# A two-level Winograd matmul with GELU: late groups taken two at a time on one block of A

## The chip, the cores and the metric

The kernel runs on one core of a Trainium2 chip. The metric is the device time of the kernel in microseconds (us), the median of several runs. A core has TensorE (PE: matmuls; PEld: loads of their stationary operand), VectorE (DVE), ScalarE (ACT), GpSimd (POOL) and SyncE (SP). GpSimd and SyncE issue the transfers here. Matmuls add up into PSUM, which has 8 banks of 128 x 512 float32; all other tiles lie in SBUF.

## The reference

```python
a: 4096 x 4096 float32, b: 4096 x 4096 float32
x = np.matmul(a, b)
return 0.5 * x * (1 + np.tanh(np.sqrt(2 / np.pi) * (x + 0.044715 * x**3)))
```

A full product of two square matrices, and GELU (tanh form) of each element. The kernel rounds A and B to fp16 and checks their sizes on the way; a slower general path stands behind that check and is not taken with these inputs.

## The kernel before

**Two levels of Winograd's scheme.** A is cut into four quadrants A11 to A22, and so is B. Seven products P1 to P7 of quadrants or of sums of quadrants give the four quadrants of the output:

```
S1 = A21+A22   S2 = S1-A11   S3 = A11-A21   S4 = A12-S2
T1 = B12-B11   T2 = B22-T1   T3 = B22-B12   T4 = B21-T2
P1 = A11*B11   P2 = A12*B21  P3 = S4*B22    P4 = A22*T4   P5 = S1*T1   P6 = S2*T2   P7 = S3*T3
C11 = P1+P2    U = P1+P6     V = U+P5       C12 = V+P3    C21 = U+P7+P4   C22 = V+P7
```

Each quadrant of C is worked in tiles of 512 rows by 512 columns. A *group* is one tile position (mb, nb) in all four quadrants at once: 4 x 4 = 16 groups, 0 to 15, each with the seven products. A product of a group is (512 x 2048) times (2048 x 512). `products` (L558, matmul on L563) does an *uncut* one: 4 quarters of the inner dimension x 4 row tiles x 4 matmuls of 512 columns. A *cut* one is done by Winograd's scheme once more (`split`, `stage`, `part_pe`, matmul on L955): 7 parts x 2 row tiles x 8 matmuls of 256 columns. It needs sums of its A operand (`inner_sum`, L883: sums "5", "7", "6", "3"; with a *base* that an earlier group of the block has left in place only "5", "7", "3"), sums of its B operand (`made_here`, `made_stored`: four each; none for `fetched` pieces), and copies and adds of half banks between its four stages (L968, L972). The stages are: part 1; parts 2, 5; parts 6, 7; parts 3, 4. Part p writes the quadrant of the product's four banks that `WHERE` (L55) names: part 3 the right half of banks 0 and 1, part 4 the left half of banks 2 and 3, part 1 also banks 2 and 3. Where `bits` is set, the first matmul of each row tile of part 1 is widened to 512 columns.

**What is cut.** `RAW_CUT` names the cut products of the raw groups 1 to 6 (B comes from the input and its sums are made and stored, `raw_group` L1344). `GROUPS` (L117) does it for groups 7 to 15: per product f (pieces of B fetched), m (B sums made in place), ms (made and stored for later), um (uncut, pieces made), and uncut if it isn't named. `late_group` (L1530) runs them one after another. A group has eight banks as two sets X and Y; two different products, such as P1 on X and P2 on Y, run interleaved stage by stage (`both`, L1627). Results leave the banks by ScalarE copies (L1166), VectorE adds (`add_bank`, L1172) and GELU (L1150). A cut P4 at the end of some groups is held back (`pending`) and run beside the next group's P1 or P4.

**Memory.** SBUF is managed by hand as 28 *cells* of 128 x 2048 fp16 (512 KB): 0 to 15 are B's four slots, 16 to 19 are called SB, 20 to 23 SA, 24 to 27 ST (the staging tiles), beside four slots of four cells for A's raw quadrants, and 15 *smalls* of 128 x 512 float32. In the late groups SA holds S1, ST holds S3, and S2 and S4 lie in SB and in A21's slot; the 16 cells of B serve fetches, B sums and inner A sums. When a row block changes (groups 7 and 11), `turn_quad` (L1185) loads the next block of A, transposes it on VectorE and sums squares on ScalarE (L1206).

**The order of the work.** Every operation is first put on record with its engine, an assumed cost (`COST`, `MOVE`), what it reads and what it writes. `Plan.schedule` (L206) then plays the program through with these costs: TensorE takes its operations in the order of the program, and each other engine takes the ready operation that is due first, waiting for a nearly ready one that is due sooner. `LAG` (0.2 us) is added between engines, and `MARGIN` (0.6 us) behind a transfer that VectorE or ScalarE waits for. `emit` writes the instructions in that order, and on the chip each engine keeps to it.

Of the kernel before, what the change touches and what calls it, by code (L numbers as in the profile page):

```python
# [16 lines left out]
P = 128  # L17
# [50 lines left out]
MARGIN = 0.6  # L68
# [21 lines left out]
def modes_of(tail=None, early=None, first4=None, **kw):  # L90
    got = {name: mode for mode, names in kw.items() for name in names.split()}
    return {**got, **{k: v for k, v in (("tail", tail), ("early", early), ("first4", first4)) if v}}


def bases_of(all_modes):
    got = {}
    for gs in (tuple(range(N_RAW, 8)), (8, 9, 10, 11), (12, 13, 14, 15)):
        early = [g for g in gs if all_modes[g].get("early") == "start"]
        turn = gs[-1] in TURNS
        for name in NAMES:  # L100
            if turn and (name in ("P2", "P6") or early and name in ("P1", "P5")):
                continue
            own = [g for g in gs if not (name == "P3" and (g in TURNS or g in early))]
            found = []
            while own and all_modes[own[-1]].get(name, "u") in ("f", "m", "ms"):
                found.append(own.pop())
            if len(found) > 1:
                for g in found:
                    got[g, name] = "made"
                got[found[-1], name] = "make"  # L110
    return got
# [16 lines left out]
TURNS = {7: 2, 11: 3}  # L128
# [191 lines left out]
def half_path(  # L320
# [105 lines left out]
    def turn_a(quad, c, h=None):  # L426

        x = slice(0, NX) if h is None else slice(h * NX // 2, (h + 1) * NX // 2)
        if (quad, c) == THIRD:
            n = NX // RT  # L430
            parts = [(slice(i * n, (i + 1) * n), staged[quad, c][i]) for i in range(x.start // n, x.stop // n)]
        else:
            parts = [(x, staged[quad, c][:, x, :])]
        for x, src in parts:
            transpose(a_slot[quad], c, x, src)

    def transpose(slot, c, x, src):
        dst = a_phys[slot, c].bitcast(U32).rearrange("p jj (mb q) -> p jj mb q", q=Q)
# [368 lines left out]

    def new_small():
        return free_small.pop(0)
# [21 lines left out]
    def fetch_unit(nb, name, q):  # L831
        x = new_cell()
        dma("POOL", cell(x), unit(nb, name)[:, q, :], [("u", nb, name, q)], [c(x)], "unit")
# [16 lines left out]


# [31 lines left out]
    def inner_sum(op, x, y, t=None):  # L883
        t = new_cell() if t is None else t
# [55 lines left out]
    def part_pe(z, p):  # L940
# [22 lines left out]
        if p in z.sum and p != "6" and z.last:  # L963
            free_cells.append(z.sum.pop(p))
# [9 lines left out]
    def stage(z, k):  # L974
# [22 lines left out]
        elif k == 2:  # L997
            part_pe(z, "2")
            x5 = z.sum["5"]
            part_pe(z, "5")  # L1000
            if z.last:
                free_cells.remove(x5)
# [182 lines left out]
    def turn_quad(mb, quad, slot, pairs):  # L1185
# [3 lines left out]
        for h in range(2):  # L1189
# [9 lines left out]
            for cc in range(CH):  # L1199
                src = s.rearrange("p x (c r) -> p c x r", c=CH)[:, cc]  # L1200
                x = slice(h * n, (h + 1) * n)
                dve("turn", lambda cc=cc, x=x, src=src: transpose(slot, cc, x, src), toks, [("a", slot, cc, h)])
            f = new_small()
            for x in range(n):
                r = h * n + x
                act("weigh", lambda x=x, r=r, s=s, f=f: nc.scalar.activation(  # L1206
                    small[f].bitcast(F16)[:, : 2 * RUN], s[:, x, :], ACT.Square, accum_out=t[:, kh, r : r + 1]),
                    toks, [("rows", ih), ("f", f)], batch=("w", mb, quad, h), slack=60.0)
            free_small.append(f)
# [134 lines left out]
    def raw_group(gi, keep_units, makes, fetch=(), next_nb=None, turn=None, pending=None):  # L1344
# [47 lines left out]
        if turn:  # L1392
# [4 lines left out]
            turn_quad(turn, "11", slots["a"]["21"], (24, 26))  # L1397
# [23 lines left out]
        if turn:  # L1421
            turn_quad(turn, "12", slots["a"]["11"], (24, 26))
# [16 lines left out]
        if turn:  # L1439
            turn_quad(turn, "21", slots["a"]["12"], (24, 26))  # L1440
# [37 lines left out]
        def p4_ends():  # L1478
            if turn:
                turn_quad(turn, "22", slots["a"]["22"], (24, 26))  # L1480
# [46 lines left out]
    sets, held_sums = {"X": 0}, []  # L1527
    BASE = bases_of(GROUPS)

    def late_group(gi, modes, turn=None, pending=None):  # L1530

        mb, nb = groups[gi]
        new_mb = gi == N_RAW or groups[gi - 1][0] != mb
        last = gi == LAST
        X, Y = sets["X"], 1 - sets["X"]
        cut = {name for name in NAMES if modes.get(name, "u") in ("f", "m", "ms")}
        p4_first = bool(turn) or "first4" in modes
        if p4_first:
            cut.discard("P4")
        tail_v = "P7" in cut or "P3" in cut and modes.get("tail") == "v" or "P4" in cut  # L1540
        tail_v = tail_v or pending is not None and not p4_first
        if gi == N_RAW:
            for q in range(QPH):
                copy_quarter(ST[q], raw("21"), q)
        elif new_mb:
            block(SA, 1, raw("21"), raw("22"))
        if new_mb or not held_sums:
            block(SB, -1, blk(SA), raw("11"))
        s3 = ST
        if new_mb and gi != N_RAW:  # L1550
            block(ST, -1, raw("11"), raw("21"))
        def early():
            k = new_unit()
            turn_quad(groups[gi][0] + 1, "11", slots["a"]["21"], (k[0], k[2]))
            free_cells.extend(k)

        held_sums.clear()
        s4_in_slot = not turn and modes.get("early") != "start"
        if modes.get("early") == "start":
            early()  # L1560
        if s4_in_slot:
            if new_mb:
                s4 = raw("21")
                for q in range(QPH):
                    dst, toks = a_quarter(s4, q)
                    combine2(dst, toks, a_quarter(raw("12"), q), a_quarter(blk(SB), q), -1)
            held_sums.append(gi)
        if turn:
            k = new_unit()
            pairs = (k[0], k[2])  # L1570

        def fourth():
            if not s4_in_slot:
                block(SB, -1, raw("12"), blk(SB))
        source = {
            "P1": raw("11"), "P2": raw("12"), "P5": blk(SA), "P6": blk(SB), "P7": blk(s3), "P3": raw("21") if s4_in_slot else blk(SB), "P4": raw("22")
        }

        def work(name, s, fresh, done=None, bits=False, lead=None, seen=None):
# [5 lines left out]
            z = split(s, source[name], b, bits, BASE.get((gi, name)), lead)  # L1585
            if seen is not None:
                seen.append(z)
            return stages_of(z, done)

        p1, u, v, y = {}, {}, {}, {}  # L1590
        alone = not {"P1", "P2"} & cut
        keep_p1 = not alone or "P6" in cut

# [24 lines left out]
        def p5_done(i):  # L1618
            if tail_v and p4_first:
# [3 lines left out]
            elif tail_v:  # L1623
                v[i] = new_small()
                add_bank(u[i], Y, i, v[i])

        def both(xs, ys):  # L1627
# [264 lines left out]
```

## Time and profile before

| | |
|---|---|
| median of 3 runs | 1497.44 us (1496.33 to 1498.01) |
| profiled execution | 1500.4 us, of which span 1498.5 us |
| mean granted clock of TensorE | 0.998 |
| moved by DMA | 388.76 MB, mean 259 GB/s |
| full-length sums of L871 on VectorE (128 x 2048 fp16) | 600 |

The span runs from the first to the last instruction of one profiled execution. "Busy" is the union of an engine's instructions; a matmul's row has its whole passage through the array as its length (379 ns for 512 columns, 273 ns for 256), while the next one starts much earlier, so that prices of matmuls are taken from start to start. A row of a group reads: line, engine, operation, output <- inputs, shape, count | busy us, mean ns of one | idle time of the engine just before, and what ended it. A row of a waiting list: engine, tile and line that waited <- what it waited for: us in all, times, longest. A row of the chain or of the timeline begins with its start and its length in us.

### The profile page before, as it was taken

To read this page: it belongs to the slowest core of one execution; us is meant where nothing else is said; L and a number is where in the kernel's file an instruction comes from. 1 tells how busy PE (TensorE), PEld (TensorE's weight loads), DVE (VectorE), ACT (ScalarE), POOL (GpSimd) and SP (SyncE) were. 2 spreads that over 40 slices of the span, in tenths; PEclk is the share of its full clock that TensorE was granted. 3 is DMA by queue.
4 is the path that set the end of the run, shared out by engine and by line. 5 is a ranking of instruction groups with operands and counts; after the bars stand their busy time and mean duration, and the time that the engine had idled before them with its cause. 6 is when DMAs were issued, how large, how long until landed. Compare 5 with 4: busy or idle time off the path is not lost.

```text
span 1498.5 us, 26219 instructions
## 1 busy us (share of the span) xinstructions
PE 1483.8 (99%) x9886; PEld 967.4 (65%) x9886; DVE 1207.5 (81%) x1476; ACT 708.8 (47%) x1606; POOL 452.6 (30%) x822
## 2 busy tenths in 40 slices
PE   9999999999999999999999999999999999999997
PEld 4444554444445446555665888887765778888886
DVE  2598778246499889686799999998699889998887
ACT  5445246363954645546663242436654234242433
POOL 7766342451204415212330212122331112112220
PEclk9999999999999999999999999999999999999999
DMA  9999799999979999997997777889997747698974
GB/s 177 193 204 224 135 247 314 292 279 268 249 269 250 284 356 254 309 264 239 252 330 297 269 265 241 299 272 215 305 283 288 259 141 264 209 336 279 327 257 182
DMA packets 200918, 388.76 MB, mean 259 GB/s; under 512 B 20304, under 2 KB 110416, under 8 KB 200784
## 3 DMA queue, kind: packets, MB, share of 16 engines
q0 software_dynamic: 139296, 231.79, 65.3%
q1 hardware_dynamic: 61488, 155.22, 27.5%
q8 instruction: 79, 1.29, 0.3%
q14 instruction: 55, 0.45, 0.1%
HBM read 315.62 MB, written 155.19 MB: 314 GB/s over the span
## 4 chain that ended last, share of the span: by engine, by line
PE 90%; DMA 5%; POOL 2%; DVE 1%; ACT 1%; issue 1%; DVEq 0%; ACTq 0%; POOLq 0%
PE acc L563 47%; PE acc L955 43%; DMA stage<-in_a_dram 2%; DMA bR<-k_unit 2%; POOL bR L465 1%; POOL stage L465 1%; DVE bR L871 0%; POOL aD L465 0%; DVE y L1172 0%; DMA out_dram<-y 0%; ACT stage L474 0%; DMA aD<-in_a_dram 0%; DMA bR<-in_b_dram 0%; ACT y L1150 0%; ACT y L1206 0%
## 5 line engine op out<-in xcount | busy, mean ns | idle before, releaser
L563 PE MATMUL acc<-bR,aT 128*128 128x512 f16 x1792 | 393.6, 379 | 1.0 <-DVE y L1172 0.6
L871 DVE TENSOR_TENSOR bR<-bR 128x2048 f16<-128x2048 f16 (+1 forms) x292 | 344.7, 1203 | 47.1 <-PE acc L955 23.6
L789 POOL DMA_DIRECT2D bR<-k_unit x258 | 143.7, 559 | 629.7 <-PE acc L955 359.3
L563 PE MATMUL acc<-bR,aD 128*128 128x512 f16 x1472 | 322.4, 379 | 0.0
L563 PEld LDWEIGHTS <-aT 128*128 128x128 f16 x1856 | 181.6, 98 | 215.0 <-issue 1.6
L955 PE MATMUL acc<-bR 128*128 128x256 f16 x2640 | 307.3, 273 | 1.5 <-ACT y L968 1.5
L955 PEld LDWEIGHTS <-bR 128*128 128x128 f16 x2640 | 258.3, 98 | 33.6 <-issue 1.6
L563 PEld LDWEIGHTS <-aD 128*128 128x128 f16 x1568 | 153.3, 98 | 182.5 <-DVE aD L548 1.2
L1172 DVE TENSOR_TENSOR y<-acc,y 128x512 f32<-128x512 f32 x324 | 209.0, 684 | 36.0 <-ACT y L1166 14.7
L789 POOL DMA_DIRECT2D bR<-in_b_dram x288 | 155.5, 545 | 252.5 <-DMA bR<-in_b_dram 102.2
L955 PE MATMUL acc<-bR,aT 128*128 128x256 f16 (+1 forms) x1696 | 201.0, 274 | 0.0
L968 ACT COPY y<-acc 128x256 f32<-128x256 f32 x220 | 81.6, 372 | 238.2 <-PE acc L955 235.4
L955 PEld LDWEIGHTS <-aT 128*128 128x128 f16 x1696 | 166.0, 98 | 24.4
L1150 ACT ACTIVATE y<-y 128x512 f32<-128x512 f32 x200 | 119.9, 626 | 109.0 <-DVE y L1172 108.7
L1240 ACT ACTIVATE y<-bR 128x1024 bf16<-128x1024 f16 x128 | 129.8, 1052 | 66.0 <-DVE y L1245 51.9
L1245 DVE TENSOR_TENSOR y<-y 128x1024 bf16<-128x1024 bf16 x120 | 82.1, 686 | 41.6 <-ACT y L1240 40.1
L955 PE MATMUL acc<-bR,aD 128*128 128x256 f16 (+1 forms) x944 | 110.9, 273 | 0.0
L955 PE MATMUL acc<-bR,stage 128*128 128x256 f16 (+1 forms) x880 | 105.7, 274 | 0.0
L955 PEld LDWEIGHTS <-aD 128*128 128x128 f16 x944 | 92.4, 98 | 12.1
L955 PEld LDWEIGHTS <-stage 128*128 128x128 f16 x880 | 86.1, 98 | 15.1
L871 DVE TENSOR_TENSOR bR<-aT 128x2048 f16<-128x2048 f16 x66 | 80.3, 1217 | 18.2 <-PE acc L563 18.2
L1166 ACT COPY y<-acc 128x512 f32<-128x512 f32 x80 | 45.9, 586 | 103.2 <-PE acc L563 65.4
(89 smaller groups left out, 1223.4 us busy)
## 6 DMA issues: line engine op xcount, KB each, us to landing
bR<-k_unit POOLq DMA_DIRECT2D x258, 512.0 KB, 7.0
out_dram<-y SPq DMA_DIRECT2D x252, 256.0 KB, 7.0
k_unit<-bR SPq DMA_DIRECT2D x112, 512.0 KB, 8.8
bR<-in_b_dram POOLq DMA_DIRECT2D x384, 128.0 KB, 6.9
k_piece<-bR SPq DMA_DIRECT2D x40, 512.0 KB, 4.7
bR<-in_a_dram POOLq DMA_DIRECT2D x64, 256.0 KB, 8.9
stage<-in_a_dram POOLq DMA_DIRECT2D x48, 256.0 KB, 7.7
bR<-k_piece POOLq DMA_DIRECT2D x24, 512.0 KB, 7.7
```

The source lines that it names most:

```text
L465: nc.gpsimd.dma_start(out=dst, in_=src)
L563: nc.tensor.matmul(acc, sa[:, j // 2, i * P : (i + 1) * P, j % 2], sb[:, j, :], start=start and j == 0, stop=stop and j == 3, skip_group_c ...
L789: return plan.add(queue, COST[queue], lambda: eng.dma_start(out=dst, in_=src), r=r, w=w, size=MOVE[what] * SPREAD, weight=weight, **kw)
L871: nc.vector.tensor_tensor(out=dst, in0=xa, in1=ya, op=ALU.add if op > 0 else ALU.subtract)
L955: nc.tensor.matmul(PS[s][i][:, :] if wide else PS[s][i][:, w * HC : (w + 1) * HC], sa[:, j // 2, r * P : (r + 1) * P, j % 2], rhs(j, wide) ...
L968: act(cost, lambda: nc.scalar.copy(out=d, in_=x), [xt] if xt else [], [dt])
L1150: act("gelu", lambda: nc.scalar.activation(t, t, ACT.Gelu_apprx_tanh), [("f", f)], [("f", f)])
L1166: act("copy", lambda: nc.scalar.copy(out=sm(f), in_=bank(s, i)), [], [("f", f), ("p", s, i)])
L1172: dve("add", lambda: nc.vector.tensor_tensor(out=sm(g), in0=bank(s, i), in1=sm(f), op=ALU.add), [("f", f)], [("f", g), ("p", s, i)])
L1240: act("square", lambda t=t, src=src: nc.scalar.activation(t, src, ACT.Square), [c(cx)], [("f", f)], slack=60.0)
L1245: dve("add16", lambda t=t, u=u: nc.vector.tensor_tensor(out=u, in0=u, in1=t, op=ALU.add), [("f", f)], [("f", e)], slack=60.0)
```

## The change

Groups 8 to 15 are taken as four pairs, (8,9), (10,11), (12,13), (14,15), by a new function `late_pair`; `late_group` becomes `lone_group` and is left for group 7 alone. Both groups of a pair have the same rows of A. The pair goes through P1, P2, P6, P5, P3, P7, P4, and at each step runs that product of both groups interleaved, the first group on bank set 0 and the second on bank set 1. Where both are cut, they share the A sums: the first makes "5" and "7", the second makes "6" over the cell of "5", and "3" over "6"; the second group runs part 5 before part 2. Bases are kept for P4 and P7 alone. S2 is made at the start of each pair in one place and overwritten by S4 ahead of P5. S3 takes A21's slot, so the four staging cells and the rest, 20 cells, are free for B; three of them (`EXTRA`) become six more smalls, which leaves 17. In three pairs (`PARK`) U is stored to DRAM ahead of P3 and fetched back ahead of P7. The next block of A is turned in groups 7 and (10,11), into whichever block is done with. The tables of what is cut are new, and `MARGIN` is 0.2 instead of 0.6. Group 7 no longer copies S3 into the staging cells (L877).

```diff
-MARGIN = 0.6
+MARGIN = 0.2
...
 def bases_of(all_modes):
     got = {}
...
+    for a, b in ((8, 10), (12, 14)):
+        for name in ("P4", "P7"):
+            if all(all_modes[g].get(name, "u") in ("f", "m", "ms") for g in (a, a + 1, b, b + 1)):
+                got[a, name], got[b, name] = "make", "made"
     return got
...
-RAW_MAKES = {4: ("P1", "P4", "P3"), 5: ("P2",)}
-RAW_CUT = {4: "P7", 5: "P7 P3", 6: "P7", 2: "", 1: "P7"}
+RAW_MAKES = {4: ("P1", "P4"), 5: ("P4",), 6: ("P3",)}
+RAW_CUT = {4: "P3", 5: "P3", 6: "P7", 2: "", 1: "P3"}
 GROUPS = {
-    7: modes_of(m="P1 P6", ms="P7", tail="v"),
-    8: modes_of(f="P7", m="P3 P4 P6", ms="P5", um="P2"),
-    9: modes_of(f="P3", m="P1 P4 P5 P6 P7", ms="P2"),
-    10: modes_of(m="P1 P2 P3 P5 P7", ms="P6", early="end"),
-    11: modes_of(m="P1 P2 P6 P7", tail="v"),
-    12: modes_of(m="P4 P6 P7", ms="P5", tail="v"),
-    13: modes_of(f="P7", m="P1 P2 P3 P4 P5 P6"),
-    14: modes_of(f="P3", m="P2 P6 P7", ms="P1 P4 P5"),
-    15: modes_of(f="P2 P6", m="P1 P4 P5 P7", ms="P3", tail="v", first4=True),
+    7: modes_of(m="P1 P5 P6", um="P2 P4", tail="v"),
+    8: modes_of(m="P1 P2 P3 P4 P6 P7", ms="P5"),
+    9: modes_of(m="P4 P5 P7", ms="P2 P6", um="P3"),
+    10: modes_of(f="P4", m="P1 P2 P3 P6", ms="P5"),
+    11: modes_of(m="P1 P2 P3 P4 P5"),
+    12: modes_of(f="P3", m="P1 P4 P5 P6 P7", ms="P2"),
+    13: modes_of(f="P4", m="P1 P2 P5 P7", ms="P3 P6"),
+    14: modes_of(f="P3", m="P4 P7", ms="P1 P2 P5 P6"),
+    15: modes_of(f="P4", m="P1 P2 P5 P6 P7", ms="P3"),
 }
+EXTRA = (13, 14, 15)
+OWN = True
+TWO = True
+TEMPS = ()
+SLACK = 60.0
+PARK = (8, 12, 14)
-TURNS = {7: 2, 11: 3}
+TURNS = {7: 2, 10: 3}
...
         elif k == 2:
-            part_pe(z, "2")
             x5 = z.sum["5"]
-            part_pe(z, "5")
+            for p in "25" if z.first else "52":
+                part_pe(z, p)
...
+    def late_pair(ga, turn):
+
+        gs = (ga, ga + 1)
...
+        if groups[ga - 1][0] != mb:
+            fill("S1", 1, "21", "22")
+            fill("S2", -1, "S1", "11")
+            at["S3"] = at["21"]
+            fill("S3", -1, "11", "21")
+        else:
+            fill("S2", -1, "S1", "11")
...
+        def both(name, fresh, dones, bits):
+            lists, cuts, lead = [], [], None
+            for s in range(2):
+                gi, mode = gs[s], GROUPS[gs[s]].get(name, "u")
...
+                b = {"f": fetched, "m": made_split, "ms": made_stored}[mode](nb, name)
+                shared = is_cut(0, name) and is_cut(1, name)
+                z = split(s, source[name], b, bits(s), BASE.get((ga, name)) if shared else None, lead)
+                lead = z if shared else None
+                lists.append(stages_of(z, lambda i, s=s: dones(s, i)))
+                cuts.append(s)
...
+        def p7_done(s, i):
+            add_bank(v[s][i], s, i)
+            if is_cut(s, "P4"):
+                add_bank(u[s][i], s, i)
+            out_of(gs[s], i, 1, 1, v[s][i])
...
+        both("P1", lambda s: True, p1_done, uncut("P2"))
+        new_a("11", "11")
...
+        both("P2", cut("P2"), p2_done, uncut("P6"))
+        both("P6", cut("P6"), p6_done, uncut("P5"))
...
+        fill("S2", -1, "12", "S2")
+        new_a("21", "12")
+        both("P5", cut("P5"), p5_done, uncut("P3"))
+        if ga in PARK:
+            park()
+        new_a("22", "S1")
+        both("P3", cut("P3"), p3_done, lambda s: False)
+        new_a("12", "S2")
+        if ga in PARK:
+            unpark()
+        both("P7", lambda s: True, p7_done, uncut("P4"))
+        both("P4", cut("P4"), p4_done, lambda s: False)
...
-        for gi, modes in GROUPS.items():
...
-            pending = late_group(gi, modes, TURNS.get(gi), pending)
+        lone_group(N_RAW, TURNS[N_RAW])
+        more_smalls()
...
+        for gi in range(N_RAW + 1, LAST, 2):
...
+            late_pair(gi, TURNS.get(gi))
```

The functions of the diff that are left out: `seed` copies a small into a bank where the next product of that group is uncut and goes on in it; `park` and `unpark` move the eight tiles of U to DRAM (SP) and back (POOL); `fill` makes one A block by four sums; `new_a` calls `turn_quad`, which with `OWN` writes its squares over the staging cell that it has read.

More of the change, by code (lines that the diff above doesn't have):

```diff
@@ L1525, in raw_group @@
         return later_
-    sets, held_sums = {"X": 0}, []
     BASE = bases_of(GROUPS)
[L1530 to L1535, printed above, removed]
-        cut = {name for name in NAMES if modes.get(name, "u") in ("f", "m", "ms")}
[L1537 to L1574, printed above, removed]
@@ new lines, in lone_group @@
+        turn_quad(turn, "11", raw("11"), pairs)
+        both(("P6", X, False, p6_done, not tail_v), ("P5", Y, True, p5_done, not tail_v))
+        block(SB, -1, raw("12"), blk(SB))
+        turn_quad(turn, "21", raw("12"), pairs)
+        turn_quad(turn, "12", blk(SA), pairs)
+        if tail_v:
+            both(("P7", X, True, c22_v, True), ("P3", Y, True, c12))
+            for i in range(RT):
+                c21(i)
+        else:
+            run(work("P7", X, False, c22))
+            for i in range(RT):
+                c21(i)
+            run(work("P3", Y, False, c12))
```

359 lines of the change are left out of this document (178 added, 181 removed).

## The prediction

> **What bounds the kernel now.** I read the page first, then who TensorE waited for, then the chain that ended last, then the groups of instructions with shapes kept apart, then single stretches of the timeline.
>
> ```profile
> span 1498.5 us, 26219 instructions
> PE 1483.8 (99%) x9886; PEld 967.4 (65%) x9886; DVE 1207.5 (81%) x1476; ACT 708.8 (47%) x1606; POOL 452.6 (30%) x822
> ```
> ```profile
> PE acc L955 <- ACT y L968: 1.5, 1, 1.5
> ...
> PE acc L563 <- DVE y L1172: 0.6, 1, 0.6
> ...
> PE acc L563 <- DMA bR<-k_unit: 0.4, 1, 0.4
> ```
> ```profile
> 201.07 265.91 PE acc L563 x1232
> ...
> 676.31 3.49 PE acc L955 x32
> ...
> 1219.51 253.03 PE acc L955 x2304
> ```
>
> TensorE is busy for all but 14.7 of 1498.5 us. The three waits shown are all those behind the first 100 us: 2.5 us. The chain is matmuls nearly throughout. It also gives their price: 265.91/1232 = 0.2158 us for a matmul of 512 columns (L563), 3.49/32 = 0.1091 us for one of 256 (L955). So the time is the number of matmuls, plus whatever new waiting there is.
>
> An uncut product is 4 quarters x 4 row tiles x 4 = 64 wide matmuls: 64 x 0.2158 = 13.81 us. A cut one is 7 parts x 2 row tiles x 8 = 112 narrow ones: 112 x 0.1091 = 12.22 us. Two of these are widened to 512 columns where `bits` is set, at 0.1067 us extra each, 0.21 us per product.
>
> ```profile
> L563 PE MATMUL acc<-bR,aT 128*128 128x512 f16 x1792 | 393.6, 379 | 1.0 <-DVE y L1172 0.6 <-DMA bR<-k_unit 0.4
> L563 PE MATMUL acc<-bR,aD 128*128 128x512 f16 x1472 | 322.4, 379 | 0.0
> L955 PE MATMUL acc<-bR 128*128 128x256 f16 x2640 | 307.3, 273 | 1.5 <-ACT y L968 1.5
> L955 PE MATMUL acc<-bR,aT 128*128 128x256 f16 x1672 | 198.6, 273 | 0.0
> L955 PE MATMUL acc<-bR,aD 128*128 128x256 f16 x942 | 110.7, 273 | 0.0
> L955 PE MATMUL acc<-bR,stage 128*128 128x256 f16 x866 | 103.8, 273 | 0.0
> ...
> L563 PE MATMUL acc<-aD 128*128 128x512 f16 x96 | 21.4, 379 | 1.1 <-DVE aD L548 0.7 <-ACT y L581 0.4
> L563 PE MATMUL acc<-aD,aT 128*128 128x512 f16 x64 | 14.1, 379 | 0.0
> ...
> L955 PE MATMUL acc<-bR,aT 128*128 128x512 f16 x24 | 9.1, 379 | 0.0
> L955 PE MATMUL acc<-bR,stage 128*128 128x512 f16 x14 | 5.3, 379 | 0.0
> L955 PE MATMUL acc<-bR,aD 128*128 128x512 f16 x2 | 0.8, 379 | 0.0
> ```
>
> The reader is to check my counting of the code on these. L955 sums to 6120 narrow and 40 wide matmuls, 6160 = 55 cut products, 20 of them widened. The tables say the same: 5 cut in the raw groups, 50 in groups 7 to 15. L563 has 3424.
>
> **The change part by part: TensorE.** I count the new tables in the same way. Raw groups: P3 in 1, 4 and 5, P7 in 6, so 4. Lone group 7: P1, P5, P6. Groups 8 to 15: 7, 5, 6, 5, 7, 7, 7, 7. That is 54 late, 58 in all: three more products are cut. Widening falls from 20 products to 8, because a pair's cut product is widened only if the same group's next product is uncut: 4 raw, 2 in group 7, P5 of group 9, P2 of group 11.
>
> So 3 x 64 = 192 wide matmuls of L563 go and 24 of L955's 40 wide ones become narrow: 216 x 0.2158 = 46.6 us less. 336 + 24 = 360 narrow ones come: 360 x 0.1091 = 39.3 us more. **TensorE's work: -7.4 us.**
>
> **VectorE.** Its largest group gives the length of a full sum, 1.22 us, and a stretch near the end the distances.
>
> ```profile
> L871 DVE TENSOR_TENSOR bR<-bR 128x2048 f16<-128x2048 f16 x284 | 339.8, 1218 | 47.1 <-PE acc L955 23.6 <-PE acc L563 9.2 <-DMA bR<-in_b_dram 6.4
> ```
> ```profile
> 1474.83 1.22 DVE L871 TENSOR_TENSOR bR<-aT 128x2048 f16<-128x2048 f16 x1
> ...
> 1475.85 1.91 PE L955 MATMUL acc<-bR,stage 128*128 128x256 f16 x16
> 1475.97 1.22 DVE L871 TENSOR_TENSOR bR<-bR 128x2048 f16<-128x2048 f16 x1
> ...
> 1477.11 1.22 DVE L871 TENSOR_TENSOR bR<-stage 128x2048 f16<-128x2048 f16 x1
> ...
> 1477.60 1.91 PE L955 MATMUL acc<-bR 128*128 128x256 f16 x16
> ...
> 1478.24 1.09 DVE L972 TENSOR_TENSOR acc<-acc,y 128x256 f32<-128x256 f32 x3
> ...
> 1484.30 7.33 DVE L1172 TENSOR_TENSOR y<-acc,y 128x512 f32<-128x512 f32 x12
> ...
> 1488.08 1.91 PE L955 MATMUL acc<-bR,aT 128*128 128x256 f16 x16
> ```
>
> Back to back, sums start 1.14 us apart (1474.83, 1475.97, 1477.11), bank adds take 7.33/12 = 0.61 each in a row, half-bank adds 1.09/3 = 0.36. Full sums in groups 7 to 15: S2 and S4 for each pair make the A blocks 56 instead of 44; the inner A sums, now made once for both groups of a pair, 117 instead of 172; B sums 196 instead of 176; together 369 instead of 392. There are 16 more half-length B sums, 16 more half-bank adds and 4 fewer bank adds. VectorE loses work on the whole.
>
> The fullest pair, (12,13), has 16 + 28 + 48 = 92 sums, 56 bank adds and 56 half-bank adds: 105 + 34 + 20 = 159 us. Its 14 cut products take TensorE 171 us, so VectorE is filled to 93%.
>
> ```profile
> 850.00:900.00 50.00, 50.00 (x458) 44.62 (x457) 49.37 (x63) 20.83 (x49) 8.39 (x16) 1.00 0.72 247
> ...
> 1100.00:1150.00 50.00, 48.52 (x309) 30.04 (x307) 47.09 (x60) 27.76 (x70) 14.08 (x26) 1.00 1.01 312
> ```
>
> The columns are TensorE, weight loads, VectorE, ScalarE, GpSimd, granted clock, DMA. VectorE at 49.37 of 50 us already leaves TensorE full. I cost its changes at nothing; matmuls hide them, and this pair would have to gain 12 us of VectorE work before they show as a sum.
>
> [...]
>
> **Waits that are new.** These the totals do not show. In the old order the two interleaved products had their own A sums; between part 5, which frees the cell of sum 6, and part 6, which needs it, lay the other product's two parts, 3.49 us. Now both groups use one sum. Sum 6 waits for part 5 of the second group, and one part later, 1477.60 - 1475.85 = 1.75 us, the first group's part 6 wants it. Sum 3 stands so between part 6 of the second group and part 3 of the first, again one part apart. Swapping parts 2 and 5 is what leaves even that.
>
> ```profile
> 589.50 0.69 DVE L1172 TENSOR_TENSOR y<-acc,y 128x512 f32<-128x512 f32 x1 [0.38 <-DMA out_dram<-y]
> ...
> 590.25 1.02 PE L563 MATMUL acc<-bR,aT 128*128 128x512 f16 x4 [0.60 <-DVE y L1172]
> ```
> ```profile
> 1121.81 0.38 PE L955 MATMUL acc<-bR 128*128 128x256 f16 x2
> ...
> 1122.03 3.62 PE L563 MATMUL acc<-bR,aD 128*128 128x512 f16 x16
> ...
> 1122.23 1.22 DVE L871 TENSOR_TENSOR bR<-bR 128x2048 f16<-128x2048 f16 x1 [0.33 <-PE acc L955]
> ```
>
> VectorE starts 0.20 us after the next matmul does (1122.03 to 1122.23). TensorE follows VectorE by 0.06 us (589.50 + 0.69 to 590.25). A weight load goes about 0.1 us ahead of its matmul. The chain is 0.20 + 1.22 + 0.06 + 0.10 = 1.58 us in 1.75: it fits with 0.17 us over if VectorE is free at that moment. Products that both groups cut and that keep no base: P2, P5, P6, P7 in (8,9); P1, P2, P3, P5 in (10,11); P1, P2, P3, P5, P6 in each later pair. That is 18, with two such places each: 36 windows. Behind a late sum queue the other group's B sums and bank adds, and TensorE waits for those next. Price: 0 if each is met; (1.14 - 0.17) x 36 = 35 us if one other sum always goes first. The nearest row is the old late waiting, 2.5 us in 63 products with VectorE as full; I keep that and add 1.0 us. The low end is -2.5 us, should the old waits go too.
>
> **The rest, at nothing.** The last matmul starts at 1489.7 or so, and adds and GELUs follow as now: the new end has 8 adds in the last stages, not 12, worth 0 to -0.6 us. Of three pairs, 24 tiles of 256 KB are parked by SP and fetched back by GpSimd.
>
> ```profile
> L789 POOL DMA_DIRECT2D bR<-k_unit x258 | 143.7, 559 | 629.7 <-PE acc L955 359.3
> ```
> ```profile
> bR<-k_unit POOLq DMA_DIRECT2D x258, 512.0 KB, 7.0
> out_dram<-y SPq DMA_DIRECT2D x252, 256.0 KB, 7.0
> bR<-in_b_dram POOLq DMA_DIRECT2D x384, 128.0 KB, 6.9
> ```
>
> Eight fetches push later B units back by 8 x 0.56 = 4.5 us on GpSimd's queue. That queue has long idle times, and 17 free cells now serve two products of 8 cells with shared sums: it hides; without that cover, 3 x 4.5 = 13 us. The planner's smaller margin (0.2 instead of 0.6 us after a landing) costs between nothing and 0.4 us for each first B sum, 12 of them in the fullest pair: 4.8 us of VectorE time against 12 us spare. I take nothing. In raw groups 1, 4 and 5 the next B12 is now released only with B22, at the group's end: 32 issues x 0.56 = 17.9 us + 6.9 = 24.8 us, where the next P5 comes 2 x 13.8 = 27.6 us later. It just fits; if not, I bound it at 3 x 3 us.
>
> **Sum.** The profiled execution took 1500.4 us (span 1498.5). 1500.4 - 7.4 + 1.0 = 1494.0. The median of the runs, 1497.44, lies 0.2% below that execution; in its scale 1494.0 is **1491.0 us**.
>
> **Rivals.** All start from 1490.0, the median less 7.4 us.
>
> First, slower: **the 36 windows are missed**. One VectorE sum is ahead of the shared one in half of them: 18 x 0.97 = 17.5 us, 1507.5. It breaks even at 0.20 us lost per window. For it: VectorE works in order, is 93% full, and has 0.17 us to spare. Against it: at 49.37 of 50 us it holds TensorE up nowhere between 850 and 900 us, and shared sums make its queue shorter.
>
> Second, no change: **banks drain late before P4**. Where P7 and P4 are cut in both groups (three pairs), 16 bank adds, 16 x 0.61 = 9.8 us, follow P7; from the first free bank (1.75 + 0.20 us into the first group's last stage) to part 1 of the second group's P4 (five parts, 8.75 us) there are 6.8. The missing 3.0 us cost 0 if the banks wanted first go first, 9.0 us in three places if the order is bad; half, 4.5, gives 1494.5.
>
> Third, no change: the raw loads come late, 1490.0 + 9 = 1499.
>
> Fourth, slower: many short waits drop the granted clock. At half clock the 36 parts behind the windows take another 36 x 1.75 = 63 us, 1553. Against it: 1.5 us of waiting in the row 1100 to 1150 left the clock at 1.00. [...]
>
> **How the numbers follow.** Forecast 0.60, windows 0.22, banks 0.12, raw loads 0.03, clock 0.03. About 0.2%, 3 us, can be told from no change: faster is below 1494.4 (0.60), within it banks and loads (0.15), slower windows and clock (0.25). The forecast's own range runs from 1487.0 (1490.0 with the old waits and 0.6 us of the end gone, rounded) to 1494.4. The range goes on over the banks' 9.0 us (1499.0) to the middle of the windows' case, where 15 us are lost: 1505. It leaves out the worse half of that, the clock, and a little below.
>
> **What would show it.** Right: L955 with 6496 matmuls, 16 of them wide, L563 with 3232, VectorE's L871 with 569 full sums, and TensorE's waits behind 100 us together near 3.5 us. Wrong: TensorE waiting for VectorE's sums dozens of times by 0.2 to 1 us (first rival); three waits of 1 to 3 us for bank adds ahead of P4 (second); a wait for loads of B from HBM in the first 600 us (third); a granted clock under 1.00 in late rows (fourth). A changed price of a matmul would break the sum itself.

## The result and the profile after

The changed kernel takes 1489.3 us in the median of 9 runs (1487.42 to 1492.96), the kernel before 1498.25 us beside it (1496.33 to 1502.47). The ratio is 0.994, with a 95% interval of 0.9927 to 0.9953: 9 us faster. The prediction said 1491.0, 6.4 us faster, in a range of 1487 to 1505.

The profiled execution took 1489.25 us. First its page, line 1 and the busy time.

```profile
span 1487.7 us, 26622 instructions
PE 1476.8 (99%) x10030; PEld 981.3 (66%) x10030; DVE 1170.0 (79%) x1445; ACT 709.9 (48%) x1642; POOL 464.3 (31%) x843
```

The span is 10.8 us shorter, TensorE has 144 more matmuls (narrower ones) and 7.0 us less busy time, VectorE 37.5 us less. L955 is now L964, L563 is L559, L871 is L879, L1172 is L1182, L968 is L978, L972 is L982.

Next, of the groups with shapes kept apart, the two that hold widened matmuls, and of the chain its longest piece.

```profile
L964 PE MATMUL acc<-bR,aD 128*128 128x512 f16 x12 | 4.5, 379 | 0.0
L964 PE MATMUL acc<-bR,aT 128*128 128x512 f16 x4 | 1.5, 379 | 0.0
```
```profile
1115.16 366.81 PE acc L964 x3360
```

16 wide ones, as counted. All groups of L964 together hold 6496 matmuls, those of L559 3232; L879 has 569 full sums. These are the numbers forecast. L982 has 232 adds, four for each of 58 cut products. The long piece gives 366.81/3360 = 0.1092 us for a narrow matmul: its price is unchanged (0.1091). 3360 matmuls are 30 cut products: for 367 us TensorE does not stop, through P4 of (10,11) and all seven products of the two pairs behind it.

Who TensorE waited for, the three rows behind 100 us:

```profile
PE acc L964 <- DVE bR L879: 1.0, 1, 1.0
...
PE acc L964 <- DMA bR<-k_unit: 0.5, 1, 0.5
PE acc L964 <- ACT y L978: 0.3, 1, 0.3
```

Three waits again, 1.8 us instead of 2.5. The 1.0 us is one of the 36 windows of the prediction, missed. In the timeline:

```profile
1069.84 1.23 DVE L879 TENSOR_TENSOR bR<-bR 128x2048 f16<-128x2048 f16 x1 [2.05 <-DMA bR<-k_unit]
...
1070.47 1.91 PE L964 MATMUL acc<-bR,aD 128*128 128x256 f16 x16
...
1072.11 1.22 DVE L879 TENSOR_TENSOR bR<-bR,aD 128x2048 f16<-128x2048 f16 x1
...
1073.39 2.79 PE L964 MATMUL acc<-bR 128*128 128x256 f16 x24 [1.01 <-DVE bR L879]
```

VectorE had stood 2.05 us for a transfer; the shared sum (bR<-bR,aD) came third behind that one and ended at 1073.33; TensorE went on 0.06 us later. This is how the first rival looks. It happened once. A window that is met, in pair (8,9):

```profile
821.24 1.91 PE L964 MATMUL acc<-bR,aD 128*128 128x256 f16 x16
821.44 1.23 DVE L879 TENSOR_TENSOR bR<-bR,aD 128x2048 f16<-128x2048 f16 x1 [0.52 <-PE acc L964]
...
822.99 7.15 PE L964 MATMUL acc<-bR 128*128 128x256 f16 x64
```

VectorE stands idle, starts 0.20 us into the part between, and is done 0.32 us before TensorE needs the sum; with the 0.06 us for the hand-over, 0.26 are left. All 20 windows of the last two pairs are met in this way: 0.25 or 0.26 us are left in 19 of them and 0.13 in one, and in 17 VectorE stood idle just before.

The end of the timeline: the last 16 matmuls, the last bank add, the stores. The row of the kernel before is the one that answers to the stores.

```profile
1480.05 1.91 PE L964 MATMUL acc<-stage,aT 128*128 128x256 f16 x16
...
1480.76 2.95 SPq L785 DMA_DIRECT2D out_dram<-y  x4
...
1482.00 0.69 DVE L1182 TENSOR_TENSOR y<-acc,y 128x512 f32<-128x512 f32 x1 [0.18 <-PE acc L964]
```
```profile
1485.67 7.47 SPq L789 DMA_DIRECT2D out_dram<-y  x12
```

The last matmul's slot ends at 1480.05 + 1.75 = 1481.8, the span 5.9 us later. Before it was 1488.08 + 1.75 = 1489.8 and 8.7 us. So the 10.8 us are 8.0 before the last matmul and 2.8 behind it.

The same split for every run, in us. A wait counts 0.16 more than its row shows, since a narrow matmul's row ends 0.16 us after the next one could have started (0.273 against 0.109).

| kernel | ratio to before (95%) | last matmul ends | waits behind 100 us | from there to the end |
|---|---|---|---|---|
| before | 1 | 1489.8 | 3, 3.0 | 8.7 |
| changed | 0.994 (0.9927 to 0.9953) | 1481.8 | 3, 2.3 | 5.9 |
| three uncut | 0.9974 (0.9962 to 0.9986) | 1489.9 | 2, 4.6 | 6.0 |
| P7 last | 1.0001 (0.9992 to 1.0009) | 1486.3 | 6, 5.9 | 12.7 |
| part 2 first | 1.0143 (1.0128 to 1.0157) | 1512.0 | 22, 31.6 | 5.8 |
| own sums | 1.0467 (1.0452 to 1.0482) | 1557.7 | 44, 59.9 | 7.3 |
| margin 0.6 | 0.9975 (0.9964 to 0.9986) | 1486.0 | 7, 5.8 | 6.5 |
| before, margin 0.2 | 1.0035 (1.0019 to 1.0051) | 1498.9 | 8, 10.3 | 8.6 |
| two queues | 0.9944 (0.9928 to 0.9959) | 1484.3 | 3, 2.0 | 6.1 |
| raw P7 too | 1.0133 (1.0115 to 1.0152) | 1510.2 | 20, 27.5 | 6.2 |
| margin 0.4 | 0.9967 (0.9955 to 0.9979) | 1483.8 | 3, 4.3 | 6.2 |
| margin 0 | 0.9986 (0.9974 to 0.9997) | 1485.4 | 4, 4.3 | 7.4 |
| S2 twice | 1.0153 (1.014 to 1.0166) | 1513.9 | 18, 27.2 | 7.6 |
| two more cut | 1.0099 (1.0086 to 1.0112) | 1506.3 | 17, 24.9 | 6.5 |

The ratios come from 4 to 12 runs of a kernel, the other columns from one profiled execution of it. Executions of one kernel lie 3 to 11 us apart, so a column shows where the time of that execution went, not the mean of all. What is left of the third column without the fourth is called TensorE's own work below: 1486.8 before, 1479.5 in the changed kernel. It still holds the waits of the first 100 us, 1.9 to 5.2 us.

### The profile page after: what moved, and what is told of

It reads as the page before. It is cut to its first block, busy times and chain, and to the rows that moved or that the text cites. A ratio compares the mean times of both kernels' runs of the same rounds, so it can differ in the third digit from the quotient of the medians.

```text
span 1487.7 us, 26622 instructions
## 1 busy us (share of the span) xinstructions
PE 1476.8 (99%) x10030; PEld 981.3 (66%) x10030; DVE 1170.0 (79%) x1445; ACT 709.9 (48%) x1642; POOL 464.3 (31%) x843
## 4 chain that ended last, share of the span: by engine, by line
PE 89%; DMA 5%; DVE 2%; POOL 2%; issue 1%; ACT 1%; ACTq 0%; DVEq 0%; POOLq 0%
PE acc L559 45%; PE acc L964 44%; DMA stage<-in_a_dram 2%; DMA bR<-k_unit 1%; DMA out_dram<-y 1%; DVE bR L879 1%; DMA bR<-in_b_dram 1%; POOL bR L461 1%; DMA k_piece<-stage 1%; POOL stage L461 1%; DMA aD<-in_a_dram 0%; ACT stage L470 0%; DVE y L1182 0%; POOL bR L785 0%; POOL aD L461 0%
## 5 line engine op out<-in xcount | busy, mean ns | idle before, releaser
L559 PE MATMUL acc<-bR,aT 128*128 128x512 f16 x1760 | 385.9, 379 | 0.0
L559 PEld LDWEIGHTS <-aT 128*128 128x128 f16 x1856 | 181.6, 98 | 213.7
L964 PEld LDWEIGHTS <-bR 128*128 128x128 f16 x2800 | 273.9, 98 | 34.2 <-DVE bR L879 1.3
L879 DVE TENSOR_TENSOR bR<-bR 128x2048 f16<-128x2048 f16 (+1 forms) x221 | 253.8, 1169 | 47.4 <-PE acc L559 18.8
L559 PE MATMUL acc<-bR,aD 128*128 128x512 f16 x1248 | 272.3, 379 | 0.0
L559 PEld LDWEIGHTS <-aD 128*128 128x128 f16 x1376 | 134.5, 98 | 162.4 <-DVE aD L544 1.5
L785 POOL DMA_DIRECT2D bR<-k_unit x199 | 110.3, 557 | 414.8 <-PE acc L964 155.9
L964 PE MATMUL acc<-bR 128*128 128x256 f16 x2000 | 232.1, 273 | 1.0 <-DVE bR L879 1.0
L964 PEld LDWEIGHTS <-aT 128*128 128x128 f16 x1808 | 176.9, 98 | 22.8
L1182 DVE TENSOR_TENSOR y<-acc,y 128x512 f32<-128x512 f32 x222 | 144.8, 684 | 41.4 <-ACT y L1176 17.6
L978 ACT COPY y<-acc 128x256 f32<-128x256 f32 x180 | 66.3, 372 | 195.5 <-PE acc L964 182.0
L964 PE MATMUL acc<-bR,aT 128*128 128x256 f16 (+1 forms) x1360 | 159.5, 273 | 0.0
L1160 ACT ACTIVATE y<-y 128x512 f32<-128x512 f32 x149 | 91.2, 630 | 84.3 <-DVE y L1182 83.3
L964 PEld LDWEIGHTS <-aD 128*128 128x128 f16 x1168 | 114.3, 98 | 17.3 <-issue 0.7
L964 PE MATMUL acc<-bR,aD 128*128 128x256 f16 (+1 forms) x864 | 102.6, 274 | 0.5 <-DMA bR<-k_unit 0.5
L436 DVE STREAM_TRANSPOSE aT<-stage 128x1024 uint32<-128x1024 uint32 (+1 forms) x39 | 50.0, 1309 | 64.9 <-DMA stage<-in_a_dram 31.0
L964 PE MATMUL acc<-stage,bR 128*128 128x256 f16 x800 | 92.9, 273 | 0.0
L1217 ACT ACTIVATE y<-stage 128x512 f16<-128x512 f16 x128 | 80.5, 629 | 20.7 <-DMA stage<-in_a_dram 12.6
```

Source lines behind the costliest of these rows:

```text
L436: nc.vector.transpose(dst[:, :, x, :], src)
L559: nc.tensor.matmul(acc, sa[:, j // 2, i * P : (i + 1) * P, j % 2], sb[:, j, :], start=start and j == 0, stop=stop and j == 3, skip_group_c ...
L785: return plan.add(queue, COST[queue], lambda: eng.dma_start(out=dst, in_=src), r=r, w=w, size=MOVE[what] * SPREAD, weight=weight, **kw)
L879: nc.vector.tensor_tensor(out=dst, in0=xa, in1=ya, op=ALU.add if op > 0 else ALU.subtract)
L964: nc.tensor.matmul(PS[s][i][:, :] if wide else PS[s][i][:, w * HC : (w + 1) * HC], sa[:, j // 2, r * P : (r + 1) * P, j % 2], rhs(j, wide) ...
L978: act(cost, lambda: nc.scalar.copy(out=d, in_=x), [xt] if xt else [], [dt])
```

## The experiments

My theory: fewer matmuls give most of the gain, VectorE keeps up because a pair shares its A sums and just meets the windows, and a shorter end gives the rest. The rival: the new order and its margin give the gain by fewer waits, and the number of matmuls has little to do with it.

**Three products uncut again.** P2 of group 9, P3 and P5 of group 11 run uncut.

```diff
-    9: modes_of(m="P4 P5 P7", ms="P2 P6", um="P3"),
+    9: modes_of(m="P4 P5 P7", ms="P6", um="P3 P2"),
-    11: modes_of(m="P1 P2 P3 P4 P5"),
+    11: modes_of(m="P1 P2 P4"),
```

> The changed kernel with three products uncut again (P2 of group 9, P3 and P5 of group 11), nothing else. If the number of matmuls sets the time: 3 x (13.81 - 12.22) = 4.8 us more than the changed kernel, about 1494 beside 1498 before, ratio 0.997. If the gain came from the new order and its waits and not from matmuls: no change, ratio 0.994, since VectorE even loses 12 B sums.

Ratio 0.9974, that is 0.0034 x 1498 = 5.1 us above the changed kernel; 4.8 were forecast. The ratio alone does not show that matmuls are what is paid for: another order alone cost 4 to 7 us (the margin, below), and this execution has one long wait that the changed kernel has not, with a lower clock around it.

```profile
PE acc L964 <- ACT acc L978: 4.1, 1, 4.1
```
```profile
740.00:750.00 10.00, 5.89 (x42) 4.58 (x40) 5.78 (x5) 5.91 (x19) 2.29 (x4) 0.83 1.14 301
```

The table tells them apart. Without the waits the last matmul ends at 1485.3 here and at 1479.5 in the changed kernel: 5.8 us of TensorE's own work, of which the clock of 0.83 in those 10 us is at most 1.7. The kernels with all the cut products and only another margin have 1479.5 to 1481.1 there. So the three products cost some 4 to 6 us in this execution, and the rival, for which nothing should have moved, falls.

**P7 behind P4 in the last pair.** 16 tiles are finished at the end instead of 8. `p4_first` adds P4 into U; `p7_last` adds P7 into V and U and stores both.

```diff
-        both("P7", lambda s: True, p7_done, uncut("P4"))
-        both("P4", cut("P4"), p4_done, lambda s: False)
+        if last:
...
+            y4 = ({}, {})
+            both("P4", lambda s: True, p4_first, lambda s: False)
+            both("P7", lambda s: True, p7_last, lambda s: False)
+        else:
+            both("P7", lambda s: True, p7_done, uncut("P4"))
+            both("P4", cut("P4"), p4_done, lambda s: False)
```

> The changed kernel, but the last pair runs P4 ahead of P7, so that 16 bank adds instead of 8 stand at the very end. If the end got shorter because fewer bank adds follow the last matmuls: the adds (16 x 0.61 = 9.8 us from 2 us into the last stages, which last 7 us) end 4.8 us behind the last matmul instead of 0.9, so 3.9 us more, ratio 0.9965. If the shorter end was only the landing of the last transfers: within 1 us of the changed kernel, ratio 0.994.

Ratio 1.0001: the whole gain is gone, 9 us and not 3.9. Its timeline at the end:

```profile
core 0 of [0], span 1499.0 us
...
1484.59 1.91 PE L964 MATMUL acc<-bR,aD 128*128 128x256 f16 x16
...
1486.42 3.67 DVE L1182 TENSOR_TENSOR y<-acc,y 128x512 f32<-128x512 f32 x6
...
1490.55 4.24 SPq L785 DMA_DIRECT2D out_dram<-y  x6
```

The adds end at 1490.1, 3.8 us behind the last matmul, where 4.8 were worked out. But SyncE is still issuing stores at 1494.8, one every 0.7 us (six in 4.24 us), and the span ends at 1499.0. Two stretches of this end, and the busiest one behind the last matmul of the changed kernel; the last two columns are the busy share of the DMA engines and GB/s:

```profile
1488.00:1490.00 2.00, 0.00 (x0) 0.00 (x0) 2.00 (x4) 2.00 (x4) 0.00 (x0) 1.00 1.03 380
1494.00:1496.00 2.00, 0.00 (x0) 0.00 (x0) 0.00 (x0) 0.00 (x0) 0.00 (x0) 0.50 1.03 390
```
```profile
1482.00:1484.00 2.00, 0.00 (x0) 0.00 (x0) 0.69 (x1) 1.11 (x2) 0.00 (x0) 1.00 0.77 279
```

With 16 tiles the DMA engines are full (a share of 1.03 in both stretches). A tile of 256 KB at 380 GB/s takes 0.69 us, about the distance at which SyncE issues the stores. With 8 tiles they are not full (0.77). So the end grows with the tiles that are finished in it: 8 tiles 5.9 us, 12 tiles 8.7, 16 tiles 12.7, roughly 0.85 us a tile (the versions with 8 tiles have 5.8 to 7.6). The other part is more waiting ahead of the end, 3.6 us in this execution (1.9 of it a wait for ScalarE at 1450).

**Two queues for the last stores.** The added end of `p4_done` makes the GELU of every second of the last eight tiles and stores it from ScalarE's queue.

```diff
         def p4_done(s, i):
-            add_bank(u[s][i], s, i)
-            out_of(gs[s], i, 1, 0, u[s][i])
+            f = add_bank(u[s][i], s, i)
+            if not last or i % 2 == 0:
+                out_of(gs[s], i, 1, 0, f)
+                return
...
+            plan.add("ACT", 0.1, lambda: nc.scalar.dma_start(out=out[r0 : r0 + P, c0 : c0 + NC], in_=t),
...
```

> The changed kernel, but of the last eight output tiles every second one is stored by ScalarE's queue instead of SyncE's. Kernels with 8, 12 and 16 tiles at the end took 5.9, 8.7 and 12.7 us behind the last matmul, some 0.85 us for each tile. If SyncE's issues are what takes the 0.85 us: 1 to 2 us less, ratio 0.993. If the stores share one rate however they are issued: no change, ratio 0.994.

```profile
1479.73 5.96 SPq L785 DMA_DIRECT2D out_dram<-y  x4
...
1482.52 1.91 PE L964 MATMUL acc<-stage,aT 128*128 128x256 f16 x16
...
1485.85 0.34 ACTq L1784 DMA_DIRECT2D out_dram<-y  x1
```

The last matmul ends at 1484.3, the span at 1490.4: 6.1 us, as with one queue, and the ratio is 0.9944. With 8 tiles SyncE's issuing is not what the end waits for: with either number of queues the last store is issued some 1.6 us behind the last matmul (1485.85 against 1484.3 here, 1483.4 against 1481.8 in the changed kernel, where the last GELU ends at 1483.35). How two queues would do behind 16 tiles, where the stores do pile up, no run shows.

**The window of sum 6 closed.** Part 2 ahead of part 5 in both groups.

```diff
-            for p in "25" if z.first else "52":
+            for p in "25":
```

> The changed kernel with part 2 ahead of part 5 in both groups, so that the window of the shared sum 6 closes: part 6 of the first group follows part 5 of the second at once. If shared sums are on TensorE's path: a chain of about 1.5 us at each of 18 products, 27 us more, ratio 1.012, with TensorE waiting for VectorE's sums 18 times. If sums hide wherever they stand: no change, ratio 0.994.

Of the waiting list the largest row, and one of its places in the timeline.

```profile
PE acc L964 <- DVE bR L879: 22.5, 17, 1.4
```
```profile
874.68 1.91 PE L964 MATMUL acc<-bR 128*128 128x256 f16 x16
...
876.62 1.23 DVE L879 TENSOR_TENSOR bR<-bR,aT 128x2048 f16<-128x2048 f16 x1
...
877.91 1.92 PE L964 MATMUL acc<-stage,bR 128*128 128x256 f16 x16 [1.32 <-DVE bR L879]
```

Part 5 ends its slots at 876.43, the sum starts at 876.62 and ends at 877.85, part 6 starts at 877.91: 0.19 + 1.23 + 0.06 = 1.48 us, the chain of the prediction without its 0.10 us for a weight load (the row of the load starts at 877.90 here, 0.01 us ahead of the matmul). Behind 800 us there are 18 such waits, 1.3 us each in their rows (one more, of 0.9, at another place), 27 us together. Ratio 1.0143, 30 us above the changed kernel. So with the window closed the sum is on TensorE's path at all 18 products, and swapping two parts hides it.

**Own sums for each group.** No sharing, no bases: 216 inner A sums instead of 117.

```diff
-                z = split(s, source[name], b, bits(s), BASE.get((ga, name)) if shared else None, lead)
-                lead = z if shared else None
+                z = split(s, source[name], b, bits(s), None, lead)
+                lead = None
```

> The changed kernel with A sums of its own for each group of a pair and no bases: 216 inner A sums in groups 7 to 15 instead of 117. If VectorE's room is what sharing bought: pairs (8,9), (12,13), (14,15) need 182, 191, 182 us of VectorE beside 172, 171, 171 us of TensorE, about 40 us more in all, ratio 1.02. If VectorE is no limit: within 3 us of the changed kernel, ratio 0.994 to 0.996, or faster, as the tight windows are gone.

Ratio 1.0467, 79 us above the changed kernel, twice the 40 forecast. From its waiting list and its stretches:

```profile
PE acc L964 <- DVE acc L982: 13.9, 11, 3.8
PE acc L964 <- DMA stage<-k_unit: 10.4, 5, 3.6
PE acc L964 <- DMA bR<-k_unit: 9.6, 6, 4.0
PE acc L964 <- DVE stage L879: 8.3, 6, 3.8
PE acc L964 <- DVE bR L879: 8.0, 12, 2.7
```
```profile
1100.00:1150.00 50.00, 46.12 (x271) 27.59 (x269) 38.50 (x51) 29.23 (x78) 15.98 (x27) 0.93 1.00 303
1150.00:1200.00 50.00, 42.30 (x363) 36.36 (x362) 45.30 (x55) 19.48 (x48) 7.35 (x14) 0.94 0.64 223
```

TensorE waits for sums, for adds and for fetches. Some waits last over 3.5 us (3.52 us in the first of these stretches, 3.56 and 3.81 in the second), and there the granted clock falls to 0.93 and 0.94. The matmuls take longer as well: 3.38 us for the 16 narrow ones behind the wait of 3.52 us, 0.211 each, where 0.109 is the price. Of the 77 us between the two profiled executions, 58 are waits, 1 is the end and 18 are TensorE's own work. What sharing brings is room, and the cut products need it. Whether it is VectorE's time or the cells that the added sums take, this run does not tell apart: VectorE is busy for only 38.5 us of the first stretch, and 20 us of waiting in the rows above are for fetches. Both groups also run part 2 ahead of part 5 here, as in the run before.

**The margin, both ways.** MARGIN 0.6, 0.4 and 0 in the changed kernel, 0.2 in the kernel before.

```diff
-MARGIN = 0.2
+MARGIN = 0.6
```

> The changed kernel with MARGIN 0.6 as before. If the margin is worth nothing, as costed: ratio 0.994, within 1.5 us of the changed kernel. If planning closer to the landings is part of the gain: 2 us or more of it go, ratio 0.9955 or above. If the one wait of 1.0 us that followed a late landing is the margin's price: it goes, ratio 0.993.

> The kernel before with MARGIN 0.2 and nothing else. If the margin is worth nothing: ratio 1.000 within 0.001. If it is part of the gain: ratio 0.998 or below. If the old order, with fewer free cells, has its transfers later: slower, ratio above 1.001.

> The changed kernel with MARGIN 0.4. The margin turned out to matter with opposite signs: 0.6 costs the changed kernel 5 us, 0.2 costs the old one 5 us. If the time follows the margin: halfway, 2 to 3 us above the changed kernel, ratio 0.9955 to 0.996. If each margin gives another order with waits of its own, and the tables were picked with 0.2: anywhere from 0.994 to 0.998, with the waits in other places than at 0.6.

> The changed kernel with MARGIN 0. If the time follows the margin (smaller is better): 0 to 2 us below the changed kernel, ratio 0.993. If operations then stand too close behind late landings, or if any other order is worse than the one the tables were picked with: 2 to 6 us above it, ratio 0.996 to 0.998.

Ratios 0.9975, 0.9967, 0.994 and 0.9986 at 0.6, 0.4, 0.2 and 0; and 1.0035 for the old kernel at 0.2. There is no trend: 0.2 is best in the new kernel and worse in the old, and any other value costs the new one 4 to 7 us. Some waits stand in new places, some come back with another length: the one for a ScalarE copy near 926 us is 0.3 us in the changed kernel, 1.2 at 0.6 and 1.8 at 0.4, and the missed window costs 1.2 us at 0. The largest in three of them, from the waiting lists of 0.6, of 0.4 and of the old kernel at 0.2:

```profile
PE acc L964 <- DVE y L1182: 1.6, 1, 1.6
```
```profile
PE acc L964 <- ACT y L978: 1.8, 1, 1.8
```
```profile
PE acc L955 <- DMA bR<-k_piece: 2.8, 1, 2.8
```

So the margin has no price of its own that these runs show. Another margin gives another order, and each of the two kernels runs best in the order of its own constant. That the tables were picked for it fits, but is only argued. With one margin in both kernels the change would have gained 3.7 us at 0.6 (0.9975) and 14 us at 0.2 (0.994 against 1.0035); the measured 9 us belong to the two constants as well as to the pairs.

**S2 made twice.** The prediction held 12 us of VectorE per pair to be spare; this takes 4.6 of them.

```diff
+        for _ in range(1):
+            fill("S2", -1, "S1", "11")
         source = {
```

> The changed kernel with S2 made twice at the start of each pair: 16 more full sums, 4.6 us of VectorE per pair. If VectorE has the 12 us per pair to spare that the prediction counted: nothing but another order, 0 to 3 us, ratio 0.994 to 0.996. If VectorE's work is on the path already: 4 x 4.6 = 18 us, ratio 1.006.

Ratio 1.0153, 32 us above the changed kernel, for 18 us more VectorE work. Both theories of the expectation fall: it is far from nothing, and more than the work itself. The longest wait, at the start of pair (12,13), and the clock around it:

```profile
1166.38 2.35 DVE L879 TENSOR_TENSOR aT<-aT 128x2048 f16<-128x2048 f16 x2
...
1168.98 3.48 DVE L879 TENSOR_TENSOR aD<-aT,aD 128x2048 f16<-128x2048 f16 x3
...
1172.39 2.35 DVE L879 TENSOR_TENSOR aT<-aT 128x2048 f16<-128x2048 f16 x2
...
1174.99 1.22 DVE L879 TENSOR_TENSOR bR<-bR,stage 128x2048 f16<-128x2048 f16 x1
...
1176.26 3.57 PE L964 MATMUL acc<-bR,aT 128*128 128x256 f16 x16 [6.10 <-DVE bR L879]
```
```profile
1165.00:1340.00 175.00, 166.81 (x1502) 147.89 (x1501) 155.28 (x201) 63.36 (x147) 37.23 (x66) 0.97 0.80 286
```

VectorE makes seven sums of A blocks ahead of the B sum that TensorE stands for. In this stretch VectorE itself is busy for only 155 of 175 us. By the table the 33.8 us between the two profiled executions are 24.9 of waits, 7.2 of TensorE's own work at the lower clock (0.97 here, 0.98 from 1340 to 1515 us), and 1.7 at the end.

**Two more products cut.** P7 of groups 10 and 11.

```diff
-    10: modes_of(f="P4", m="P1 P2 P3 P6", ms="P5"),
-    11: modes_of(m="P1 P2 P3 P4 P5"),
+    10: modes_of(f="P4", m="P1 P2 P3 P6 P7", ms="P5"),
+    11: modes_of(m="P1 P2 P3 P4 P5 P7"),
```

> The changed kernel with P7 of groups 10 and 11 cut too: 60 cut products, 17 us more VectorE work in that pair, which then has some 163 us of it beside 170 us of TensorE. If matmuls set the time: 2 x 1.6 = 3.2 us less, ratio 0.992. If the pair that also turns the next block of A, with 13 free cells, cannot fetch B's units in time: TensorE waits for fetches between 980 and 1150 us, ratio 0.995 or above.

```profile
1168.19 4.62 DVE L879 TENSOR_TENSOR aD<-aT,aD 128x2048 f16<-128x2048 f16 x4
...
1174.34 3.57 PE L964 MATMUL acc<-bR,aT 128*128 128x256 f16 x16 [7.23 <-DVE bR L879]
```

Ratio 1.0099: 24 us slower than the changed kernel, not 3 faster, and the place is the same. It is no wait for fetches, as I had expected of a failure. Two matmul savings of 1.6 us each are lost many times over in 17 waits, 24.9 us together: the longest is this one of 7.2 us, the next one of 4.6 us at 1096, for a bank add in the pair (10,11) itself. Nothing here makes S2 twice, and yet VectorE again makes A sums ahead of the B sum at the start of (12,13). So that wait follows from an order that the planner reaches by more than one way; why it does is not shown.

**P7 cut in raw groups 1, 4 and 5 too.**

```diff
-RAW_CUT = {4: "P3", 5: "P3", 6: "P7", 2: "", 1: "P3"}
+RAW_CUT = {4: "P7 P3", 5: "P7 P3", 6: "P7", 2: "", 1: "P7 P3"}
```

> The changed kernel with P7 of groups 1, 4 and 5 cut as well as P3, so that P3 runs beside the next group's P1: 61 cut products. If matmuls set the time and VectorE has room in the raw groups: 3 x 1.6 = 4.8 us less, 0.6 of it lost to three more widened products, ratio 0.991. If the loads of the next B, released later by P3's running on into the next group, then come late: waits of TensorE for loads before 700 us, ratio 0.994 or above.

```profile
361.89 6.89 DVE L879 TENSOR_TENSOR bR<-bR 128x2048 f16<-128x2048 f16 x6
...
365.43 3.15 PE L559 MATMUL acc<-bR,aD 128*128 128x512 f16 x7 [4.72 <-DVE bR L879]
```

Ratio 1.0133. Four waits ahead of 700 us (1.6, 4.7, 1.6, 1.1 us) are for sums and bank adds, not for loads directly; 16 more come in the late groups, whose tables were not touched. VectorE is busy for only 50 of the 100 us from 300 to 400, so room on the whole was there. None of the versions tried beats the changed kernel.

## Why the prediction was right, and where it was off

**TensorE's work, -7.4 us: right.** Without the late waits and the end it went from 1486.8 to 1479.5 us, 7.3 less. (The terms as printed, 46.6 and 39.3, give 7.3 too; 7.4 comes from unrounded prices.) The first experiment shows the price of three products by itself, 4 to 6 us.

**New waits, +1.0 us: right in kind, too high.** 2.3 us now, 3.0 before. That all but one of the 36 windows are met was the forecast's choice between 0 and 35 us. Closing half of them shows what that costs: 27 us. The first rival was a real mechanism, and near, with 0.26 us to spare by the trace (0.17 in the forecast, which also counted 0.10 for a weight load). It went the other way because VectorE was free in time: it stood idle ahead of 17 of the 20 sums in the last two pairs.

**The end, 0 to -0.6 us: the term that was mis-sized.** It measured -2.8. I counted the adds and left out that each finished tile still has to be stored: with 8, 12 and 16 tiles the end takes 5.9, 8.7 and 12.7 us. The end (2.8 more than the sum took) and the waits (0.7 less where 1.0 more was taken) make nearly all of the difference between the forecast's 6.4 us and the 10.8 of the two profiled executions. The medians lie 9.0 apart; how the other executions divide, no trace shows.

**VectorE's changes at nothing: right for the change, wrong in its reason.** I said that the fullest pair has 12 us to spare, and its mean came out so: VectorE is busy for 161 of 171 us between 1139.5 and 1310.6. But S2 made twice, 4.6 us a pair, cost 32 us. The sum over a pair hides where the work is due. That the changed kernel fits by its order and not by the mean is what this suggests; the runs change work and order together.

**The margin at nothing: wrong as it was put.** Any other value that was tried costs 4 to 7 us, by another order. So that the number came this near is in part luck: with the old margin the same change would have gained 3.7 us, not the forecast's 6.4.

**The other rivals.** Banks before P4: no wait for a bank add in the changed kernel. Raw loads late: none there either. The clock: 0.999 in the changed kernel. 18 waits of 1.5 us, some 26 us or more apart, left it at 1.00, as in this stretch of the kernel with part 2 first.

```profile
1200.00:1300.00 100.00, 95.19 (x869) 84.45 (x867) 87.78 (x110) 31.86 (x78) 24.11 (x42) 1.00 0.86 312
```

Four short waits that stand close together did lower it. In the kernel with own sums waits of 0.3, 0.7, 0.4 and 1.6 us end between 985.8 and 992.5 us, and then:

```profile
990.00:995.00 5.00, 3.43 (x22) 2.56 (x21) 5.00 (x9) 1.26 (x3) 0.85 (x2) 0.80 0.99 340
```

The 16 narrow matmuls from 992.50 take 2.96 us there, 0.185 each instead of 0.109. Five waits of 0.3 to 0.7 us that end between 952.9 and 962.4 us in the same kernel left no such mark: the 16 narrow matmuls behind the last of them take 1.75 us, 0.109 each. So the fourth rival, whose chance of 0.03 was my estimate, is seen in this one place, and not where short waits stand apart. It was sized with half clock. A granted clock of 0.50 stands in the kernel before only behind its last matmul (1494 to 1496 us); behind short waits no run shows that (0.185 us each is the slowest found, above). Longer waits give no one answer either. In the kernel with own sums the clock is 0.93 and 0.94 in the stretches that hold its waits of 3.5 to 3.8 us. Behind a single wait of 2.6 us in the kernel with raw P7 too, 32 narrow matmuls take 5.16 us (817.20 to 822.36), 0.161 each. Behind one of 2.8 us in the old kernel at margin 0.2, 64 take 6.99 us (949.97 to 956.96), 0.109 each. What sets these two apart is not shown.

## What to carry to other kernels

Where one engine is full to 99%, count its instructions in the old and the new program: that alone gave 7.3 of the 10.8 us between the two profiled executions here. What can overturn it is not the mean load of the next engine but the few moments when it must be free, so price each hand-over that got shorter by its own chain. And a kernel whose order is planned ahead from assumed costs has to be judged with its constants: 16 more sums, or 0.2 us in a margin, give another order, and here each of these was worse.

## What the hardware showed that was not expected

The granted clock did not go by the length of a wait alone: 18 waits of 1.5 us some 26 us or more apart left it at 1.00 (part 2 first), behind four waits of 0.3 to 1.6 us within 7 us it was 0.80 from 990 to 995 us (own sums), and in stretches of 50 to 175 us with single waits of 3.5 to 6.1 us in them it was 0.93 to 0.97 (own sums, S2 twice). Eight last stores took as long from two queues (6.1 us) as from one (5.9 us); the DMA engines were not full behind one queue (share up to 0.82, in the changed kernel), and behind 16 tiles they were (1.03, at 380 and 390 GB/s).
